# First pair's weight sums, one low part and four delays of side work re-ordered in a hybrid decoder kernel

## The chip, the cores and the metric

The kernel runs on one core of a Trainium2 chip. The metric is the device time of one execution in microseconds (us), as the median of several runs. The profile is one execution taken by the hardware profiler; its times count from the start of its span.

## What is computed

One layer of a decoder trunk on 520 tokens (512 new positions of one prompt and 8 single decode tokens) with a model width of 1024: a SwiGLU feed-forward of width 2816 (FFN1), a token mixer of retention and gated delta rule with four heads each, and a second feed-forward (FFN2).

```python
def layer(x, ...):
    x = x + 0.5 * rmsnorm(swiglu(rmsnorm(x, ffn1_pre_g), ...), ffn1_post_g)
    m, s_ret_new, s_gdn_new, s_conv_new = token_mixer(rmsnorm(x, mix_pre_g), ...)
    x = x + rmsnorm(m, mix_post_g)
    x = x + 0.5 * rmsnorm(swiglu(rmsnorm(x, ffn2_pre_g), ...), ffn2_post_g)
    return x, s_ret_new, s_gdn_new, s_conv_new

# token_mixer
proj = h @ w_in                       # q, k, v, gates of both branches
o_r, s_ret_new = retention_chunked(q, k, v, g_ret, s_ret)
cq, s_conv_new = short_conv(conv_in, s_conv, gdn_conv_w)
o_g, s_gdn_new = gated_delta_chunked(gq, gk, gv, g_gdn, beta, s_gdn)
y = sigmoid(gate_r) * (norm(o_r) @ w_ret_branch) + sigmoid(gate_g) * (norm(o_g) @ w_gdn_branch)
y = y @ w_out
```

## The kernel before

Activations lie with the model width on the partitions, as eight tiles of 128 x 520 (`x[k]`), and every product works on two halves of 260 tokens. Each product is made in three passes on TensorE from a high and a low part of both operands (`hi*hi`, `lo*hi`, `hi*lo`, lines 294, 295 and 296 of `passes`). The weights come from memory as fp32 into a pool of two raw buffers (`load_to`, line 188); ScalarE casts the high part (`whi`, line 254) and VectorE makes the low part (`wlo`, line 255), which frees the raw buffer. All weight loads are issued by SyncE (SP), in order, so a load that waits for a raw buffer holds up what is queued behind it.

Most of the gate and up products of the two FFNs are taken two row blocks at a time, as a pair, by a scheme of seven products in place of eight (`pair`, line 630, and `seven`). It needs sums of weight blocks. Of a pair, `load_to` loads `raw` (line 197), the left blocks of two sums, `s1` and `s3` (lines 198 and 199), and `a22` (line 200). GpSimd (POOL) then adds the right blocks with two accumulating DMAs (`add_sums`, line 215), `SUM_LAG` = 6 ticks later at the earliest. `split_seven` (line 257) turns each of the seven factors into a high part on ScalarE (line 272) and a low part on VectorE (line 273), both named `w`; one further sum, `s2` (line 268), is made on VectorE from `s1` and `raw`. The factors are used in the order raw, `s3`, `s2` (from `s1`), `a22` and so on. The banks of the products are emptied by ScalarE copies (`u` line 640, `q` line 643) and, for the plain products that precede the pairs, by VectorE (`t`, line 619).

The program is written in one order by a planner in the kernel: the main loop emits matmuls and calls `tick()` (line 148) about once every six matmuls. A tick issues due sums, prefetches weights, and resumes the generators of side work. `yield n` in a generator means "go on n ticks later". Each engine runs its own instructions in the order in which they were written and waits on semaphores where its inputs are not ready. The generators that matter here:

- `post` (line 442), for one half of the tokens at the end of FFN1 and of the mixer: per `k` a product `t` on VectorE (line 474), `x += t` on POOL (line 476), then the normalised input as a high part on ScalarE (line 383) and a low part on VectorE (`xhl`, line 384). In half 0 it also calls for one weight unit at `k` = 1 (`prefetch(True, 1)`), which puts a `wlo` into this chain. `acc` (line 395) and `y` (line 498) are the output sums and copies of the product that ends beside it.
- `pre_rms` (line 405): squares and their sum on VectorE (`sq`, line 415), then `inverse_rms`: column sums on TensorE (`ss`, line 356), a root on POOL (`rs`, line 351), and the row factor spread by TensorE (`rb`, line 362).
- `gates` (line 943): the decay and beta rows, with `gc` (line 988) on TensorE.
- `gdn_head` and `inverse` (line 1251): the inverse of a triangular 64 x 64 block per chunk, by a loop on `pack` (lines 1279 and 1280) and small products (`pV`, line 1303), and then a serial recurrence over chunks (`ks`, `pu`, `pS`, `go`).
- `ret_head` (line 1082): the retention recurrence; each step copies a state from PSUM (`st`, lines 1114 and 1118) that the next product `po` (line 1110) needs.
- `finish_head` (line 1335): transposes a head's result (`tr`, line 935), multiplies it by its gate (`sg`, line 1352) and splits it into `oh` (line 1353) and `ol` (line 1354).
- `decode_gdn` (line 1466): the decode tokens, with column sums `cs` (line 1371) of squares `gsq` (line 1483).
- `finish_decode` (line 1524), called by the main loop right before a branch product `br`: per head `df` (line 1530) on VectorE, the high part on ScalarE (`oh`, line 1531), the low part on VectorE (line 1532). The second half's `br` matmuls need them. The retention branch's first `br` is at 682.79 us in the trace, that of the delta branch at 763.38 us.

`token_factors` (line 551) makes the token-side sums of the seven products, once the next input is complete and its row factors are made (`rooted`).

## Time and profile before

| what | value |
|---|---|
| median of 3 runs (lowest, highest) | 1265.58 us (1261.89, 1268.35) |
| the profiled execution | 1265.27 us, of which the span of the trace is 1263.5 us |
| TensorE (PE) busy | 1214.7 us, 96% of the span |
| VectorE (DVE) busy | 864.6 us, 68% |
| ScalarE (ACT) busy | 538.5 us, 43% |
| GpSimd (POOL) busy | 255.9 us, 20% |
| mean granted clock of TensorE | 0.977 of 2.4 GHz |
| FFN1, mixer, FFN2 | to about 385 us, to about 880 us, to the end |

TensorE is busy nearly all the time, so a time can only fall where TensorE waits or where its clock is granted at the lower of its two levels. The waits of TensorE are the view to start from, and the timelines of the engines that it waits for tell why.

### The profile page before, as it was taken

What the parts mean: (1) busy time and instruction counts of PE and PEld (TensorE: products, weight loads), DVE (VectorE), ACT (ScalarE), POOL (GpSimd) and SP (SyncE); (2) the same over time, 40 slices, a digit from 0 to 9 for tenths busy, and PEclk for the clock granted to TensorE, in tenths of its full rate; (3) what the DMA queues carried; (4) which work ended last, traced back from release to release, by engine and by line L of the source; (5) the groups of instructions that cost most, each with busy time, mean ns of one, the idle gap of its engine ahead of it and who ended that gap; (6) DMA issues with size and microseconds to landing.
All of it is one profiled execution on the core that took longest, in us unless ns stands there. A gap on an engine that the chain in (4) does not pass through costs nothing.

```text
span 1263.5 us, 25461 instructions
## 1 busy us (share of the span) xinstructions
PE 1214.7 (96%) x10073; PEld 1203.5 (95%) x10073; DVE 864.6 (68%) x1911; ACT 538.5 (43%) x1117; POOL 255.9 (20%) x378
## 2 busy tenths in 40 slices
PE   8999999999999998899999999999989999999995
PEld 7999999999999998899999999999989999999995
DVE  8888888653347887878786766547878878852224
ACT  6566555432234654213334333334645655542210
POOL 4111112000023257136401112204211111100003
PEclk8999999999999899999999999999989999999997
DMA  5677777353332233232434554322377777524321
GB/s 176 178 185 193 184 180 176 94 157 92 91 94 68 87 101 112 77 95 85 129 123 123 197 179 151 118 84 84 122 201 180 178 178 184 144 78 160 92 76 68
DMA packets 76552, 166.60 MB, mean 132 GB/s; under 512 B 14481, under 2 KB 19953, under 8 KB 76433
## 3 DMA queue, kind: packets, MB, share of 16 engines
q1 hardware_dynamic: 64144, 140.69, 34.9%
q0 software_dynamic: 12288, 24.29, 11.3%
q8 instruction: 79, 1.29, 0.4%
q14 instruction: 41, 0.33, 0.1%
HBM read 155.24 MB, written 9.70 MB: 131 GB/s over the span
## 4 chain that ended last, share of the span: by engine, by line
PE 72%; DVE 13%; DMA 4%; issue 3%; ACT 3%; POOL 3%; SPq 0%; DVEq 0%; ACTq 0%; POOLq 0%
PE sv L294 9%; PE sv L295 9%; PE sv L296 9%; PE dn L295 7%; PE dn L294 7%; PE dn L296 7%; PE p L294 5%; PE p L295 5%; PE p L296 5%; DMA s<-gu_in 3%; DVE wlo L255 2%; PE br L294 1%; PE br L295 1%; PE br L296 1%; DVE cv L1049 1%
## 5 line engine op out<-in xcount | busy, mean ns | idle before, releaser
L294 PE MATMUL p<-xhl,whi 128*128 128x260 f32 x784 | 234.5, 299 | 0.0
L295 PE MATMUL p<-xhl,whi 128*128 128x260 f32 x784 | 224.8, 287 | 0.0
L296 PE MATMUL p<-xhl,wlo 128*128 128x260 f32 x784 | 224.4, 286 | 0.0
L295 PE MATMUL dn<-hl,whi 128*128 128x260 f32 x704 | 200.1, 284 | 2.7 <-DVE hl L608 2.7
L294 PE MATMUL dn<-hh,whi 128*128 128x260 f32 x704 | 200.1, 284 | 0.4 <-ACT hh L606 0.4
L296 PE MATMUL dn<-hh,wlo 128*128 128x260 f32 x704 | 199.5, 283 | 0.0
L255 DVE TENSOR_TENSOR wlo<-raw,whi 128x1024 fp32r<-128x1024 f32 (+2 forms) x133 | 156.8, 1192 | 56.9 <-ACT whi L254 56.7
L294 PE MATMUL sv<-th,w 128*128 128x260 f32 x592 | 169.0, 285 | 3.4 <-ACT u L640 3.2
L296 PE MATMUL sv<-th,w 128*128 128x260 f32 x592 | 168.3, 284 | 0.0
L295 PE MATMUL sv<-tl,w 128*128 128x260 f32 x592 | 168.1, 284 | 0.0
L254 ACT CAST whi<-raw 128x1024 fp32r<-128x1024 f32 (+2 forms) x133 | 128.1, 979 | 59.3 <-DMA raw<-dn_in 52.0
L294 PEld LDWEIGHTS p<-xhl,whi 128*128 128x128 f32 x784 | 151.4, 193 | 0.7
L295 PEld LDWEIGHTS p<-xhl,whi 128*128 128x128 f32 x784 | 151.6, 193 | 0.1
L296 PEld LDWEIGHTS p<-xhl,wlo 128*128 128x128 f32 x784 | 151.1, 193 | 0.0
L273 DVE TENSOR_TENSOR w<-s,w 128x512 fp32r<-128x512 f32 x148 | 101.4, 689 | 52.7 <-ACT w L272 51.0
L295 PEld LDWEIGHTS dn<-hl,whi 128*128 128x128 f32 x704 | 133.3, 189 | 3.3 <-DVE hl L608 3.3
L294 PEld LDWEIGHTS dn<-hh,whi 128*128 128x128 f32 x704 | 133.2, 189 | 0.6 <-ACT hh L606 0.6
L296 PEld LDWEIGHTS dn<-hh,wlo 128*128 128x128 f32 x704 | 133.5, 190 | 0.0
L294 PE MATMUL sv<-xhl,w 128*128 128x260 f32 x444 | 126.2, 284 | 5.2 <-DVE t L619 4.6
L215 POOL DMA_DIRECT2D s<-gu_in x74 | 65.0, 977 | 320.1 <-DMA s<-gu_in 152.0
L295 PE MATMUL sv<-xhl,w 128*128 128x260 f32 x444 | 125.7, 283 | 0.0
L296 PE MATMUL sv<-xhl,w 128*128 128x260 f32 x444 | 125.4, 282 | 0.0
(364 smaller groups left out, 2891.6 us busy)
## 6 DMA issues: line engine op xcount, KB each, us to landing
raw<-gu_in SPq DMA_DIRECT2D x50, 512.0 KB, 4.6
raw<-win_in SPq DMA_DIRECT2D x49, 512.0 KB, 3.6
s<-gu_in SPq DMA_DIRECT2D x74, 256.0 KB, 5.3
s<-gu_in POOLq DMA_DIRECT2D x74, 256.0 KB, 4.9
raw<-dn_in SPq DMA_DIRECT2D x32, 448.0 KB, 3.4
a<-gu_in SPq DMA_DIRECT2D x37, 256.0 KB, 5.5
raw<-dn_in SPq DMA_DIRECT2D x16, 512.0 KB, 3.5
x<-x SPq DMA_DIRECT2D x16, 260.0 KB, 5.4
```

What stands on the lines that cost most here:

```text
L215: self.nc.gpsimd.dma_start(out=out, in_=term, accum_op=ALU.add)
L254: self.nc.scalar.copy(hi[:, ks], t[:, ks])
L255: self.nc.vector.tensor_tensor(lo[:, ks], t[:, ks], hi[:, ks].bitcast(F32), ALU.subtract)
L273: nc.vector.tensor_tensor(w[:, 1], t[i], w[:, 0].bitcast(F32), ALU.subtract)
L294: mm(ps, hi[:, k, :], xh, start=first, stop=False, skip_group_check=more)
L295: mm(ps, hi[:, k, :], xl, start=False, stop=False, skip_group_check=more)
L296: mm(ps, lo[:, k, :], xh, start=False, stop=last, skip_group_check=more)
L1049: nc.vector.scalar_tensor_tensor(out=acc, in0=cin[:, j : j + SEQ], scalar=w[:, j : j + 1], in1=acc, op0=ALU.mult, op1=ALU.add)
```

## The change

The diff has three parts; the number of instructions on each engine is the same before and after.

1. A new `begin_pair` issues `s3`, `s1` and `a22` of a pair and enters its two sums, `s3` first. `token_factors` calls it for the first pair of each FFN as soon as the row factors are rooted, so before the raw loads that are still to come; for all other pairs `load_to` calls it behind the pair's raw load.
2. In `post` of half 0 the one forced prefetch moves ahead of the loop over `k`, and two ticks are let pass behind it.
3. Four delays of side work grow: `pre_rms` 1 to 3 ticks, `gates` 13 to 15, `inverse` 3 to 5, `decode_gdn` 6 to 11.

```diff
             if u[0] == "seven":
                 w, m = a[f"gu{u[1]}"], u[2]
                 t = self.raw.tile([P, KD, P], F32, tag="raw", name=self.name("raw"))
-                s1, s3, a22 = (self.slot(x, (P, KH, P)) for x in ("s1", "s3", "a22"))
                 nc.sync.dma_start(out=t, in_=w[2 * m])
-                nc.sync.dma_start(out=s1, in_=w[2 * m + 1, :, 0:KH])
-                nc.sync.dma_start(out=s3, in_=w[2 * m, :, 0:KH])
-                nc.sync.dma_start(out=a22, in_=w[2 * m + 1, :, KH:KD])
-
-                self.sums_due.append((self.now + SUM_LAG, self.raw_next, s1, w[2 * m + 1, :, KH:KD]))
-                self.sums_due.append((self.now + SUM_LAG, self.raw_next, s3, w[2 * m + 1, :, 0:KH]))
+                s1, s3, a22 = self.begun.pop((u[1], m), None) or self.begin_pair(u[1], m)
...
+    def begin_pair(self, f, m):
+
+        dma, w = self.nc.sync.dma_start, self.a[f"gu{f}"]
+        s1, s3, a22 = (self.slot(x, (P, KH, P)) for x in ("s1", "s3", "a22"))
+        dma(out=s3, in_=w[2 * m, :, 0:KH])
+        dma(out=s1, in_=w[2 * m + 1, :, 0:KH])
+        dma(out=a22, in_=w[2 * m + 1, :, KH:KD])
+
+        g = self.group[self.unit_list.index(("seven", f, m, 0))]
+        self.sums_due.append((self.now + SUM_LAG, g, s3, w[2 * m + 1, :, 0:KH]))
+        self.sums_due.append((self.now + SUM_LAG, g, s1, w[2 * m + 1, :, KH:KD]))
+        return s1, s3, a22
...
         while not self.leads:
             yield 1
-        yield 1
+        yield 3
         yield from self.inverse_rms(sq[0], r, plus)
...
             self.spawn(self.pre_rms(xs, r, plus_next))
+            self.prefetch(True, 1)
+            yield 2
         lag = 2
...
-            if not hf and k == 1:
-                self.prefetch(True, 1)
             yield 1
...
         while len(xs[1]) < KD or not self.rooted:
             yield 1
+
+        self.begun[f, plain] = self.begin_pair(f, plain)
...
-        yield 13
+        yield 15
...
         nc.vector.transpose(Tc, TTc)
-        yield 3
+        yield 5
...
-        yield 6
+        yield 11
         rs = self.const("gdr", [P, 64])
```

How the order changes, in three places. The changed kernel's line numbers are 5 to 10 higher, and buffer numbers differ.

SyncE at the start of FFN2, before: the raw loads, the first copies of `x` to memory, then the first pair's raw load with its `s1`, `s3` and `a22`.

```order
L208 DMA raw_11386<-gu_in 128x1024
L208 DMA raw_11392<-gu_in 128x1024
L208 DMA raw_11637<-gu_in 128x1024
L208 DMA raw_11643<-gu_in 128x1024
L778 DMA x_11329<-x_3858 128x520
L778 DMA x_11329<-x_3859 128x520
L778 DMA x_11329<-x_3860 128x520
L778 DMA x_11329<-x_3861 128x520
L197 DMA raw_11757<-gu_in 128x1024
L198 DMA s_1900_11758<-gu_in 128x512
L199 DMA s_1901_11759<-gu_in 128x512
L200 DMA a_1902_11760<-gu_in 128x512
```

The same place in the changed kernel, where lines 211, 212 and 213 are `s3`, `s1` and `a22`:

```order
L203 DMA raw_11398<-gu_in 128x1024
L203 DMA raw_11404<-gu_in 128x1024
L211 DMA s_1863_11631<-gu_in 128x512
L212 DMA s_1862_11630<-gu_in 128x512
L213 DMA a_1864_11632<-gu_in 128x512
L203 DMA raw_11655<-gu_in 128x1024
L203 DMA raw_11661<-gu_in 128x1024
L788 DMA x_11315<-x_3858 128x520
L788 DMA x_11315<-x_3859 128x520
L197 DMA raw_11746<-gu_in 128x1024
```

The three loads have moved ahead of two plain raw loads and of the pair's own raw load, and the copies of `x` are split otherwise around that.

VectorE at the start of half 0's chain between FFN1 and the mixer (`ms` is the mean square of the rows, line 349), before:

```order
L349 SCALAR_TENSOR_TENSOR ms_4787<-ss_4782,plus_12_135 65x4
L474 TENSOR_TENSOR t_4814<-y_3692,rb_4809 128x260
L474 TENSOR_TENSOR t_4823<-y_3849,rb_4809 128x260
L255 TENSOR_TENSOR wlo_4827<-raw_4683,whi_4826 128x1024
L474 TENSOR_TENSOR t_4846<-y_4026,rb_4809 128x260
L384 SCALAR_TENSOR_TENSOR xhl_4849<-x_3858,vec,xhl_4849 128x260
```

and in the changed kernel:

```order
L357 SCALAR_TENSOR_TENSOR ms_4787<-ss_4782,plus_12_135 65x4
L263 TENSOR_TENSOR wlo_4815<-raw_4683,whi_4814 128x1024
L484 TENSOR_TENSOR t_4840<-y_3692,rb_4809 128x260
L484 TENSOR_TENSOR t_4849<-y_3849,rb_4809 128x260
L484 TENSOR_TENSOR t_4858<-y_4026,rb_4809 128x260
L392 SCALAR_TENSOR_TENSOR xhl_4861<-x_3858,vec,xhl_4861 128x260
```

The low part has left the chain and stands ahead of its first `t`.

VectorE ahead of the retention branch's decode columns, before (`tr` is the transposed result of a delta head, `rdr` and `on_dec_r` belong to the decode tokens):

```order
L1235 COPY go_8644<-go_8903 128x128
L1352 SCALAR_TENSOR_TENSOR sg_8518<-tr_8909,vec,sg_8518 128x512
L1354 TENSOR_TENSOR ol_8915<-sg_8518,oh_8914 128x512
L1379 COPY rdr_8849<-cb_8926 128x32
L1456 TENSOR_TENSOR on_dec_r<-rdo,rdr_8849 128x32
L1388 COPY vrow_8938<-tr_1463_8936 32x128
L1215 SCALAR_TENSOR_TENSOR cv_5894<-ks_8954,neg_eg,cv_5894 128x128
L802 TENSOR_TENSOR gate_8963<-p_8871,rb_5236 128x260
L802 TENSOR_TENSOR gate_8963<-p_8872,rb_5236 128x260
L1530 SCALAR_TENSOR_TENSOR df_8966<-on_dec_r,vec,sgd_7894 128x8
```

and in the changed kernel:

```order
L1245 COPY go_8676<-go_8938 128x128
L1362 SCALAR_TENSOR_TENSOR sg_8505<-tr_8944,vec,sg_8505 128x512
L1364 TENSOR_TENSOR ol_8950<-sg_8505,oh_8949 128x512
L812 TENSOR_TENSOR gate_8960<-p_8862,rb_5248 128x260
L812 TENSOR_TENSOR gate_8960<-p_8863,rb_5248 128x260
L1540 SCALAR_TENSOR_TENSOR df_8963<-on_dec_r,vec,sgd_7859 128x8
```

Four small rows that stood between `ol` and the gates now stand earlier, so the head's `sg` and `ol` come right before `df`.

TensorE at the same place, before; the head's four transposes `tr` stand above these rows, with 26 rows between:

```order
L1214 MATMUL ks_8954<-S_8643,cv_5698 128x128
L294 MATMUL p_8871<-xhl_4961,whi_8654 128x260
L295 MATMUL p_8871<-xhl_4961,whi_8654 128x260
L296 MATMUL p_8871<-xhl_4961,wlo_8655 128x260
L294 MATMUL p_8872<-xhl_5104,whi_8654 128x260
L295 MATMUL p_8872<-xhl_5104,whi_8654 128x260
L296 MATMUL p_8872<-xhl_5104,wlo_8655 128x260
L294 MATMUL br_8988<-oh_8054,whi_8760 128x260
L295 MATMUL br_8988<-ol_8055,whi_8760 128x260
L296 MATMUL br_8988<-oh_8054,wlo_8761 128x260
L294 MATMUL br_8989<-oh_8054,whi_8760 128x260
```

and in the changed kernel:

```order
L945 MATMUL tr_8944<-cst,go_7899 128x128 x4
L302 MATMUL p_8862<-xhl_4973,whi_8632 128x260
L303 MATMUL p_8862<-xhl_4973,whi_8632 128x260
L304 MATMUL p_8862<-xhl_4973,wlo_8633 128x260
L302 MATMUL p_8863<-xhl_5104,whi_8632 128x260
L303 MATMUL p_8863<-xhl_5104,whi_8632 128x260
L304 MATMUL p_8863<-xhl_5104,wlo_8633 128x260
L302 MATMUL br_8985<-oh_8047,whi_8749 128x260
L303 MATMUL br_8985<-ol_8048,whi_8749 128x260
L304 MATMUL br_8985<-oh_8047,wlo_8750 128x260
L302 MATMUL br_8986<-oh_8047,whi_8749 128x260
```

The transposes have moved to nine matmuls before the second half's `br`, the first that reads the decode columns. At the delta branch's `br` they move likewise, from 33 matmuls before it to nine.

## Rows read from the trace of the kernel before

**Rows 1.** Waits of TensorE: engine, line, releaser, us in total, times, longest.

```profile
PE sv L294 <- DVE t L619: 4.6, 1, 4.6
PE ss L356 <- DVE acc L395: 3.6, 3, 1.8
...
PE cs L1371 <- DVE gsq L1483: 3.2, 1, 3.2
...
PE pV L1303 <- DVE pack L1279: 1.5, 1, 1.5
PE ss L356 <- DVE sq L415: 1.4, 2, 1.2
```

**Rows 2.** Windows: stretch, length, busy of PE, PEld, DVE, ACT, POOL, clock, DMA.

```profile
480.00:520.00 40.00, 35.14 (x299) 34.11 (x297) 33.75 (x98) 13.05 (x35) 21.35 (x49) 0.96 0.32 96
520.00:560.00 40.00, 35.67 (x290) 34.70 (x290) 34.45 (x121) 8.65 (x18) 9.48 (x11) 0.96 0.31 98
...
929.20:933.00 3.80, 3.80 (x19) 3.80 (x19) 3.06 (x6) 3.31 (x8) 0.00 (x0) 0.50 0.93 287
```

**Rows 3.** Chain of work that ended last: start, us, what.

```profile
47.40 0.66 POOL s L215
48.06 6.73 DMA s<-gu_in
...
909.67 4.23 DMA s<-gu_in
...
915.73 6.77 DMA s<-gu_in
```

**Rows 4.** Timeline of TensorE at three waits: start, us, work, idle before, releaser.

```profile
56.35 0.58 PE L294 MATMUL sv<-th,w 128*128 128x260 f32 x1 [2.50 <-ACT u L640]
...
637.25 0.59 PE L1303 MATMUL pV<-pack,AT 32*32 32x32 f32 x16 [0.81 <-DVE pack L1293]
...
928.85 0.56 PE L294 MATMUL sv<-xhl,w 128*128 128x260 f32 x1 [4.61 <-DVE t L619]
```

**Rows 5.** Timeline of VectorE around that pair.

```profile
923.23 0.69 DVE L273 TENSOR_TENSOR w<-s,w 128x512 fp32r<-128x512 f32 x1 [5.73 <-ACT w L272]
...
928.28 0.76 DVE L619 TENSOR_TENSOR t<-g,rb 128x260 f32<-128x260 f32 x2
```

**Rows 6.** Timeline of SyncE there: two plain raw loads, the first pair's raw load.

```profile
878.79 1.53 SPq L208 DMA_DIRECT2D raw<-gu_in  x2
...
909.29 0.33 SPq L197 DMA_DIRECT2D raw<-gu_in  x1
```

**Rows 7.** Timeline of ScalarE at FFN1's second pair.

```profile
54.89 1.14 ACT L272 CAST w<-s 128x512 fp32r<-128x512 f32 x2 [2.51 <-DMA s<-gu_in]
```

**Rows 8.** Timeline of VectorE in half 0's chain after FFN1.

```profile
372.58 1.66 DVE L255 TENSOR_TENSOR wlo<-raw,whi 128x1024 fp32r<-128x1024 f32 x1
```

**Rows 9.** Timeline of GpSimd in the same chain.

```profile
372.40 6.02 POOL L476 TENSOR_TENSOR x<-x,t 128x260 f32<-128x260 f32 x6 [2.33 <-DVE t L474]
```

**Rows 10.** Timeline of VectorE before the retention branch's product.

```profile
678.53 0.75 DVE L1352 SCALAR_TENSOR_TENSOR sg<-tr,vec,sg 128x512 f32<-128x512 f32 x1
...
680.58 0.18 DVE L1379 COPY rdr<-cb 128x32 f32<-128x32 f32 x1
...
682.63 0.79 DVE L802 TENSOR_TENSOR gate<-p,rb 128x260 f32<-128x260 f32 x2
683.34 0.22 DVE L1530 SCALAR_TENSOR_TENSOR df<-on_dec_r,vec,sgd 128x8 f32<-128x8 f32 x1
```

**Rows 11.** Timeline of TensorE there.

```profile
677.89 0.60 PE L935 MATMUL tr<-cst,go 128*128 128x128 f32 x4
...
682.79 0.28 PE L294 MATMUL br<-oh,whi 128*128 128x260 f32 x1
682.91 0.28 PE L295 MATMUL br<-ol,whi 128*128 128x260 f32 x1
...
683.84 0.38 PE L294 MATMUL br<-oh,whi 128*128 128x260 f32 x1 [0.53 <-ACT oh L1531]
```

More of the change, by code (lines that the diff above doesn't have):

```diff
@@ L135, in __init__ @@
         self.sums_due = []
+        self.begun = {}
         self.hold_sums = True
@@ L549, in first_units, with token_factors @@
         return banks
-    def token_factors(self, xs, gcol, F):
+    def token_factors(self, xs, gcol, F, f, plain):
         nc = self.nc
@@ L682, in pair @@
             return banks, at
-        self.spawn(self.token_factors(xs, gpre, F))
+        self.spawn(self.token_factors(xs, gpre, F, 1 if x_from is self.a["xT"] else 2, plain))
         lead = self.first_units(xs, "g", ((0,), (1,)) if x_from is self.a["xT"] else ((0, 1), (2, 3)))
```

## Prediction

> **What bounds the kernel now.** TensorE is busy 96% of the span, so the change can win only where it waits or runs at the lower of its two clock levels. I first read the list of what TensorE waited for [rows 1]: in single places of a few us at most. The largest is one wait of 4.6 us at the first pair of FFN2; then come single waits at FFN1's second pair [rows 4], at the decode sums `cs`, at `pV` of the inverses, and at the column sums `ss`. Second, the windows of the middle [rows 2]: from 480 to 560 us TensorE is busy 35.1 and 35.7 of 40 us, VectorE 33.8 and 34.5. So there VectorE is nearly as full as TensorE, and a wait that is taken away may come back at the next value that VectorE's queue delivers. Third, the granted clock: from 929.2 to 933.0 us, right behind the 4.6 us wait, it is 0.50, which is the level of 1.2 GHz [rows 2, 4]. There 19 matmuls took 3.80 us, 0.20 each; at the level of 2.4 GHz two of the same size stand 0.12 apart [rows 11]. Such a stretch costs 19 x 0.08 = 1.5 us beside the wait itself. I use this price for all such stretches.
>
> Last I read the timelines around each wait. At FFN2's first pair VectorE's `t`, which empties a bank that TensorE needs, stands at 928.28, behind a low part `w` at 923.23 that had waited 5.73 us [rows 5]. That goes back to a sum: the load went out at 909.67 and took 4.23 us, the second accumulating DMA started at 915.73 and took 6.77 [rows 3]. The loads stand in SyncE's queue behind the raw load at 909.29 [rows 6], which has to wait for a raw buffer to come free.
>
> **The change part by part.** The sum is made against the profiled execution, 1265.3 us, of which the span is 1263.5; it is 0.3 us below the median of the runs. A positive term is a gain.
>
> *First pair of FFN2.* The three loads now come right behind two plain raw loads that were issued from 878.79 on [rows 6], nearly 30 us earlier, and the two sums follow on POOL's queue right behind the row factors, some 15 us before the 915.73 of the trace. With 4.23 us for a load and 6.77 for a sum they are in place more than 5 us before the low part of 923.23 wants them. VectorE's 5.73 us of idling goes; its rows from 923.23 to 928.28 (5.05 us) then start at about 917.5, and `t` ends at about 923.3, with its second half. TensorE came there at 928.85 - 4.61 = 924.24 [rows 4], so the whole wait goes, and with it the slow stretch: 4.6 + 1.5 = 6.1. What is late next is the second pair: its raw load still hangs on a raw buffer, and TensorE will want its `s3` sum 6 us sooner. I expect it to arrive about in time. I take 6.0, with bounds 4.0 and 7.0. On POOL nothing but later sums stands behind these two, so the 0.66 us that it spends on each [rows 3] costs nothing.
>
> On the transfers themselves no row shows the pair's loads in the earlier place. The Trainium skill (DMA: Bandwidth & Descriptors, "Issuing engines are not separate DMA queues") says that transfers started by different engines end up on the same 16 DMA engines and interleave. By that rule the early loads would lengthen the plain raw loads beside them, and lighten the crowd at 909 to 918 us; the sum stays the same as long as each is hidden.
>
> *Second pair of FFN1.* `s3` is now summed before `s1`. TensorE waited 2.5 us for `u` until 56.35 [rows 4], and `u` stood on ScalarE behind two casts at 54.89, which waited for the `s3` sum, 48.06 + 6.73 = 54.79 [rows 3, 7]. As the first of the two, it is issued at 47.40 and lands after 4.23 to 6.73 us, at 51.6 to 54.1. I take the early end, since the long ones in the rows are always the second of two. But now `s1` lands at 54.8; `s2`, its cast and the copy `q` behind it need some 1.7 us (about 0.7, 0.6 and 0.4), to 56.5 (the cast by the two of rows 7, the others are estimates from it). TensorE, not stopped at 56.35 - 2.50 = 53.85, needs `q` twelve matmuls later, 53.85 + 12 x 0.12 = 55.3: a new wait of up to 1.2. So 2.5 - 1.2, and half of a slow stretch: 2.0, bounds 0.5 and 4.0. The other pairs have the same new order, with more lead.
>
> *FFN1 to mixer.* The low part of 1.66 us at 372.58 [rows 8] leaves half 0's chain for a place where VectorE was idle, waiting for `rb`. POOL then limits: six `x += t` took 6.02 us, 1.0 each, with hardly a break [rows 9]. So not the 1.66 comes back but about 1.1. `ss` for the next row factors comes two ticks later, 12 matmuls or 1.4 us, which covers its wait of 1.2 [rows 1]. With a third of a slow stretch, 1.1 + 1.2 + 0.5 = 2.8, bounds 1.0 and 4.9. The `gates` delay of two more ticks and that of `pre_rms` cancel: the gate sums stand as far behind their rows as before, so that wait stays.
>
> *The mixer's middle.* `decode_gdn` later by five ticks (30 matmuls, 3.6 us) covers the 3.2 us wait of `cs`, and `inverse` later by two (1.4 us) just covers the 1.5 us of `pV` [rows 1]. But the next waits in this stretch, on retention's `st` and the recurrence, end with VectorE's queue, which has hardly less to do before them. VectorE idles 6.2 and 5.6 us in the two windows [rows 2], and a gain can only come out of that. Bounds are 0 and 4.7 + 1.5 = 6.2. I take 2.8, a little under the middle.
>
> *A later inverse.* The same two ticks cover the 0.8 us wait of `pV` for `pack` at 637.25 [rows 4], and most of a slow stretch behind it: 2.0, bounds 0 and 2.3.
>
> *The cost: the heads end later.* The longer inverses push the last transposes `tr` of a delta head to nine matmuls before the `br` that needs the decode columns, in both branches. In the trace `tr` starts at 677.89, `sg` 0.64 later, and VectorE is through with `ol` at 680.58, 2.69 after `tr` [rows 10, 11]. Two gates and `df` follow: 0.71 from gate to `df`, 0.50 from `df` to `br` [rows 10, 11]. That makes 2.69 + 0.71 + 0.50 = 3.90 from `tr` to `br`. TensorE has work for 0.36 (the transposes) and nine matmuls, with the change of shape some 1.5 us in all. The wait is 2.4 us where it was 0.53 [rows 11]. Twice (3.9 - 1.5 - 0.5) = 3.8, and one slow stretch for the two: -5.3. The bounds are -1.0 (other work turns out to be between) and -9.8 (1.0 more at each place for rows in VectorE's queue ahead of `sg`, and a slow stretch and a half at each).
>
> The clock level behind a wait: the 4.6 us wait has a slow stretch behind it, the 0.53 us one has not [rows 4, 2, 11]. The Trainium skill (TensorE: Matmul & The Clock Gate, "Part 1: The HAM clock gate") states that the throttled level is the default and that activity releases it. By that rule each of the two new waits could bring its own slow stretch, 1.5 more than I count; no row here shows a wait at this place long enough to tell.
>
> *Mixer to FFN2.* As at FFN1, the low part leaves the chain. The wait on `acc` there is the longest of its kind, 1.8 [rows 1], but `acc` now comes in earlier among the `t`. I take 1.2, bounds 0 and 3.3.
>
> **The sum.** 6.0 + 2.0 + 2.8 + 2.8 + 2.0 - 5.3 + 1.2 = 11.5, so 1265.3 - 11.5 = 1253.8 us.
>
> **The rivals.**
>
> A. The middle of the mixer is VectorE's: the waits at `cs` and `pV` go, and come back at `st` and the recurrence in full, and the inverse at 637 us gains nothing either. For it speaks how full VectorE is [rows 2]; against it, that it idles 12 us there. Without 2.8 + 2.0: 1258.6.
>
> B. The sums of the second pairs take over. In FFN2 the second pair's `s3` sum, like the second of the rows (6.77), arrives some 2 us late, and in FFN1 the `q` wait brings a slow stretch: 3.5 less, 1257.3.
>
> C. The two `br` waits don't come, since some product stands between. Against it speaks the order. 1253.8 - 5.3 = 1248.5.
>
> D. The change doesn't do what it says at FFN2: the early sums don't help, because the pair's own raw load, still at 909.29 [rows 6], is what is waited for. Against it, the low part of the raw block was made before VectorE fell idle. Without 6.0: 1259.8.
>
> E. Slower than before: the late heads cost more than all else gains. The place is the two `br`. If VectorE is behind with its queue when `tr` is done, each wait grows by 1.5 to 3.9, and two slow stretches follow each (3.0): 2 x (3.9 - 0.5 + 3.0) = 12.8. The same lateness would take the mixer's gains. It decides from the point where the rest brings less than 12.8; with the low ends of the FFN terms, 4.0 + 0.5, it gives 1265.3 - 4.5 + 12.8 = 1273.6.
>
> **How the numbers follow.** I give the forecast 0.47, A 0.15, B 0.10, C 0.13, D 0.09, E 0.06. The most likely time is 1253.8. A measurement of this kernel can tell about 0.5%, 6.3 us, from no change, so "faster" means below 1259.3. Forecast, C, most of B and half of A lie below: 0.47 + 0.13 + 0.08 + 0.07 = 0.75. "Slower", above 1271.9, is most of E, 0.04; the rest, 0.21, is no change. The range reaches from 1245, a few us under C since several terms have more room above than below, to 1261, just over D.
>
> **What would show it.** Right: no wait of TensorE on `t` of line 619 at the start of FFN2, and the pair's sums landed before 910 us; the casts at FFN1's second pair some 3 us earlier, with a wait of about 1 us on `q` behind them; no wait on `cs`; waits of about 2.4 us at both `br`, on the `oh` of `finish_decode`. Wrong: waits on `st` or `ks` that together are longer than before by as much as `cs` and `pV` lost (A), a wait of the FFN products on `u` or `t` one pair later (B), `br` waits near 0.5 (C), the old 5.7 us idling of VectorE at FFN2's first pair (D).

## The result, and the profile after

The changed kernel is a little slower: 1268.67 us in the median of 22 runs (1261.72 to 1274.31), beside 1265.36 us for 22 runs of the kernel before on the same chip. The ratio is 1.0029, with an interval of 1.0015 to 1.0042, so 1.9 to 5.3 us were lost where 11.5 were forecast as gained. The profiled execution of the changed kernel took 1265.6 us (span 1263.8), 3 us below its own median, so its trace shows that much less of the loss. Two executions of this study, one of the kernel before (1611 us) and one of f3_dec (2364 us), lie far above all others and are left out of every median and ratio.

First the waits of TensorE in the changed kernel; the columns are those of [rows 1]:

```profile
PE sv L302 <- ACT q L653: 5.3, 2, 3.5
PE br L302 <- ACT oh L1541: 4.3, 2, 2.2
...
PE po L1120 <- DVE st L1128: 3.0, 1, 3.0
PE po L1120 <- POOL TT L1298: 2.7, 1, 2.7
...
PE po L1121 <- DVE sT L1104: 2.0, 1, 2.0
PE sv L302 <- ACT u L650: 1.8, 1, 1.8
PE sp L1438 <- DMA sd<-sret_in: 1.7, 1, 1.7
...
PE cs L1374 <- DVE rdo L1455: 1.2, 1, 1.2
```

The rows that the change aimed at are gone: `sv` on `t` (4.6), `cs` on `gsq` (3.2) and `pV` on `pack` (1.5) of [rows 1] have no successor of more than 0.3 us. But the list is not shorter. FFN products now wait 5.3 us for `q` and 1.8 for `u` (0.2 and 3.2 before). `po` of the retention waits 7.7 us in three rows (3.2 before), `br` waits 4.3 us where it waited 1.1, and a wait on the transfer of `sd` is new.

To see in which stage this counts, the trace is cut at four groups of row factors `rb`, which TensorE spreads: those of half 0 and of half 1 behind FFN1, those ahead of FFN2, and those of half 0 behind FFN2. Before, then after, their rows (count, shortest/median/longest in ns, first to last start in us; the last row holds half 1's group too):

```profile
L362 PE MATMUL rb<-cst,rs x8: 220/275/276, 370.9 to 371.6; 65*128 65x65 f32 x8
...
L362 PE MATMUL rb<-cst,rs x8: 275/275/323, 382.8 to 383.7; 65*128 65x65 f32 x8
...
L362 PE MATMUL rb<-cst,rs x16: 221/275/276, 897.9 to 899.5; 65*128 65x65 f32 x16
...
L362 PE MATMUL rb<-cst,rs x16: 275/275/422, 1240.8 to 1250.9; 65*128 65x65 f32 x16
```

```profile
L370 PE MATMUL rb<-cst,rs x8: 221/275/275, 371.0 to 371.7; 65*128 65x65 f32 x8
...
L370 PE MATMUL rb<-cst,rs x8: 275/275/324, 381.3 to 382.1; 65*128 65x65 f32 x8
...
L370 PE MATMUL rb<-cst,rs x16: 221/275/275, 899.7 to 901.4; 65*128 65x65 f32 x16
...
L370 PE MATMUL rb<-cst,rs x16: 275/370/430, 1240.7 to 1251.3; 65*128 65x65 f32 x16
```

The stages are the differences of these starts, in us (the experiments are told below). The mixer's column holds the way into the mixer and out of it too:

| kernel | FFN1, to half 0's rb | from there to half 1's | mixer, to the rb ahead of FFN2 | FFN2, to half 0's rb | span |
|---|---|---|---|---|---|
| before | 370.9 | 11.9 | 515.1 | 342.9 | 1263.5 |
| after | 371.0 | 10.3 | 518.4 | 341.0 | 1263.8 |
| after, profiled again (e4_after) | 371.6 | 10.3 | 524.0 | 340.8 | 1269.1 |
| pairs alone (e1_pairs) | 370.5 | 12.0 | 513.9 | 340.7 | 1259.4 |
| delays alone (e3_delays) | 372.4 | 11.9 | 522.8 | 341.2 | 1271.5 |
| inverse alone (e9_inv) | 372.0 | 12.0 | 515.8 | 342.0 | 1264.2 |
| gates alone (f1_gates) | 373.8 | 12.0 | 517.9 | 342.1 | 1268.5 |
| gates and inverse (f2_gatesinv) | 372.0 | 11.9 | 524.9 | 339.4 | 1270.5 |
| decode alone (f3_dec) | 370.5 | 12.0 | 516.9 | 341.7 | 1263.5 |
| after without inverse (e6_noinv) | 371.4 | 10.2 | 515.8 | 341.6 | 1261.4 |
| two early in FFN2 (e8_twoearly) | 371.9 | 12.0 | 514.1 | 332.7 | 1253.9 |
| two early in both, low part (e12_bothtwo) | 369.8 | 10.3 | 513.4 | 333.5 | 1249.3 |

Each row is one profile, and the scatter is large: the same changed kernel has 518.4 and 524.0 us in the mixer, the profile of f1_gates lies 5 us above that kernel's median, and the kernels whose FFN2 is that of before (before, e3, e9, f1, f2, f3) have 339.4 to 342.9 there. So the 1.9 us that FFN2 gained here are within the scatter. FFN1 itself gained nothing, and the 1.6 us behind it come from the low part's move: the second column falls from 11.9 or 12.0 to 10.2 or 10.3 in every kernel that has it, and in no other. The mixer lost 3.3, in the second profile of the same kernel 8.9. So there are two questions: why FFN2 gave at most 1.9 and not 6, and what the mixer lost.

**FFN2.** The rows of the changed kernel there, engine by engine, with the idle time before an instruction and its releaser in brackets: SyncE (raw loads of the second and of the third pair), GpSimd's sums of the first and of the second pair, VectorE, ScalarE and TensorE.

```profile
920.21 0.33 SPq L197 DMA_DIRECT2D raw<-gu_in  x1
...
925.90 0.33 SPq L197 DMA_DIRECT2D raw<-gu_in  x1
...
899.11 1.86 POOL L223 DMA_DIRECT2D s<-gu_in  x2
925.16 0.86 POOL L223 DMA_DIRECT2D s<-gu_in  x1 [24.19 <-DMA s<-gu_in]
926.62 0.89 POOL L223 DMA_DIRECT2D s<-gu_in  x1 [0.60 <-issue]
...
935.12 0.69 DVE L276 SCALAR_TENSOR_TENSOR s<-s,raw 128x512 f32<-128x512 f32 x1 [3.38 <-DMA s<-gu_in]
...
935.90 0.62 ACT L280 CAST w<-s 128x512 fp32r<-128x512 f32 x1 [4.69 <-DVE s L276]
...
931.26 0.39 PE L302 MATMUL sv<-th,w 128*128 128x260 f32 x1 [1.82 <-ACT u L650]
...
936.85 0.59 PE L302 MATMUL sv<-th,w 128*128 128x260 f32 x1 [3.52 <-ACT q L653]
```

The first pair's sums go out at 899.11, long before they are wanted, and nothing waits for them. The second pair's raw load goes out at 920.21, and its two sums at 925.16 and 926.62. Beside them the third pair's raw load and three more loads run from 925.90 on. The chain of work that ended last shows what the raw load waited for, and the second sum:

```profile
918.96 1.24 DVE wlo L263
...
920.63 3.97 DMA s<-gu_in
...
926.62 8.48 DMA s<-gu_in
```

The raw load goes out as soon as the `wlo` of a plain block is made, which frees its raw buffer; the change moves nothing there. The second sum took 8.48 us, so it lands at 935.10, and VectorE's `s`, ScalarE's cast, its `q` and TensorE follow, with a wait of 3.52 us. The wait of 1.82 us before it, on `u`, comes from the first sum in the same way (4.5 us to landing). Both stand one pair later than the 4.61 us of [rows 4]. TensorE's clock fell behind the first of them and stayed low through the second. The window (columns as in [rows 2]) shows 0.50, 1.2 GHz, with 31 matmuls in it, where [rows 2] had 19:

```profile
932.40:942.60 10.20, 6.68 (x31) 6.38 (x31) 5.74 (x12) 4.36 (x10) 1.74 (x2) 0.50 0.65 138
```

In before, the second pair's raw load stood at 916.92 and the third's at 928.43, 11.5 us apart, and the second pair's second sum went out at 925.41. Their rows, and the time of that sum from issue to landing:

```profile
916.92 0.33 SPq L197 DMA_DIRECT2D raw<-gu_in  x1
...
928.43 0.33 SPq L197 DMA_DIRECT2D raw<-gu_in  x1
...
925.41 0.89 POOL L215 DMA_DIRECT2D s<-gu_in  x1 [0.49 <-ACT w L272]
...
DMA to landing us min/median/max: 4.6/4.6/4.6
```

There the third pair's loads followed 3.0 us behind the sum, which took 4.6 us. Now the raw loads are 5.7 us apart, since the first pair's raw buffer comes free earlier when that pair no longer waits, and the same sum takes 8.48. So the wait of [rows 4] had also hidden the next pair's late sums, and kept the third pair's loads off them.

**The mixer.** From 600 to 800 us, before and then after:

```profile
600.00:800.00 200.00, 198.13 (x1698) 195.56 (x1697) 141.28 (x412) 73.31 (x160) 36.77 (x63) 0.99 0.46 149
```

```profile
600.00:800.00 200.00, 192.08 (x1651) 188.87 (x1650) 137.31 (x403) 70.73 (x155) 32.40 (x57) 1.00 0.46 149
```

TensorE idled 7.9 us there instead of 1.9, at a granted clock of 1.00. Four waits make up 7.3 of it: `sp` on `sd` 1.7, `cs` on `rdo` 1.2, and the two at `br`, whose rows answer to [rows 11] and [rows 10]:

```profile
679.98 0.60 PE L945 MATMUL tr<-cst,go 128*128 128x128 f32 x4
...
683.84 0.38 PE L302 MATMUL br<-oh,whi 128*128 128x260 f32 x1 [2.17 <-ACT oh L1541]
...
680.62 0.75 DVE L1362 SCALAR_TENSOR_TENSOR sg<-tr,vec,sg 128x512 f32<-128x512 f32 x1
...
683.34 0.22 DVE L1540 SCALAR_TENSOR_TENSOR df<-on_dec_r,vec,sgd 128x8 f32<-128x8 f32 x1
```

From `tr` to `br` it is 683.84 - 679.98 = 3.86 us (3.90 forecast), and the wait is 2.17 us (2.4 forecast).

The two windows of [rows 2] in the changed kernel:

```profile
480.00:520.00 40.00, 34.98 (x283) 33.73 (x282) 36.83 (x106) 12.89 (x37) 20.14 (x48) 0.87 0.39 112
520.00:560.00 40.00, 36.20 (x311) 35.42 (x311) 31.81 (x113) 9.54 (x18) 8.46 (x11) 1.00 0.27 80
```

TensorE is busy 71.2 of 80 us, as before (70.8), though the waits on `cs` and `pV` are gone.

### The profile page after: what moved, and what is told of

Its sections match the earlier page's. It is cut to its first block, busy times and chain, and to the rows that moved or that the text cites. A ratio compares the mean times of both kernels' runs of the same rounds, so it can differ in the third digit from the quotient of the medians.

```text
span 1263.8 us, 25476 instructions
## 1 busy us (share of the span) xinstructions
PE 1210.4 (96%) x10073; PEld 1196.3 (95%) x10073; DVE 862.6 (68%) x1911; ACT 544.7 (43%) x1117; POOL 249.6 (20%) x378
## 4 chain that ended last, share of the span: by engine, by line
PE 71%; DVE 15%; DMA 4%; ACT 4%; issue 3%; POOL 1%; SPq 1%; DVEq 0%; ACTq 0%; POOLq 0%
PE sv L302 10%; PE sv L303 10%; PE sv L304 10%; PE dn L303 7%; PE dn L302 7%; PE dn L304 7%; PE p L302 4%; PE p L304 4%; PE p L303 4%; DVE wlo L263 3%; DMA s<-gu_in 2%; DVE cv L1059 1%; PE br L302 1%; PE br L303 1%; PE br L304 1%
## 5 line engine op out<-in xcount | busy, mean ns | idle before, releaser
L302 PE MATMUL p<-xhl,whi 128*128 128x260 f32 x784 | 232.3, 296 | 0.7 <-DVE S L1236 0.7
L303 PE MATMUL p<-xhl,whi 128*128 128x260 f32 x784 | 222.4, 284 | 0.5 <-DVE xhl L392 0.5
L302 PEld LDWEIGHTS p<-xhl,whi 128*128 128x128 f32 x784 | 148.7, 190 | 1.3 <-DVE S L1236 0.9
L303 PEld LDWEIGHTS p<-xhl,whi 128*128 128x128 f32 x784 | 148.9, 190 | 0.7 <-DVE xhl L392 0.7
```

The source lines that it names most:

```text
L302: mm(ps, hi[:, k, :], xh, start=first, stop=False, skip_group_check=more)
L303: mm(ps, hi[:, k, :], xl, start=False, stop=False, skip_group_check=more)
```

## The experiments

All changes are against the kernel named; ratios are against the kernel before, run on the same chip, with their 95% interval.

### Which part does what: e1, e2, e3, e4

**e1_pairs**, the kernel before with the first part alone (begin_pair, `s3` first, first pair of each FFN early):

```diff
+    def begin_pair(self, f, m):
...
+        self.begun[f, plain] = self.begin_pair(f, plain)
```

> The kernel before with part 1 alone (early first pair, s3 ahead of s1 in every pair). Theory 1, the wait moves from the first pair's t to the second pair's second sum, now s1, on which s2 and the copy q hang: no gain, 1264 to 1268 us; at FFN2's start no wait on t, but a wait on q or u of 2 to 5 us one pair later, and at FFN1's second pair a wait on q in place of u. Rival, the pairs do gain what was forecast (8 us) and the delays alone eat it: 1257 to 1259 us and no wait over 1.5 us at the second pair of FFN2.

Measured: 1260.02 us, ratio 0.9963 (0.9949 to 0.9978).

**e2_lowpart**, the kernel before with the low part's move alone:

```diff
+            self.prefetch(True, 1)
+            yield 2
...
-            if not hf and k == 1:
-                self.prefetch(True, 1)
```

> The kernel before with part 2 alone (the one low part ahead of half 0's chain, two ticks behind it). Theory 1: about 1 us gain at each of the two transitions, 1262 to 1264 us, the rest of the program as before. Rival: the two ticks and the earlier acc give it back, 1265 to 1267 us.

Measured: 1263.05 us, 0.9983 (0.9963 to 1.0002), the range of theory 1.

**e3_delays**, the kernel before with the four delays alone:

```diff
-        yield 1
+        yield 3
         yield from self.inverse_rms(sq[0], r, plus)
...
-        yield 13
+        yield 15
...
         nc.vector.transpose(Tc, TTc)
-        yield 3
+        yield 5
...
-        yield 6
+        yield 11
         rs = self.const("gdr", [P, 64])
```

> The kernel before with part 3 alone (the four longer delays). Theory 1: the middle of the mixer gains 3 to 6 us by 600 us and the late heads lose 7 us or more between 608 and 775 us, so 1266 to 1270 us, with waits of about 2.2 us at both br. Rival, the delays gain as forecast (2 to 3 us in sum): 1262 to 1263 us.

Measured: 1273.14 us, 1.0065 (1.0039 to 1.0092).

**e4_after**, the changed kernel once more beside these three:

> The changed kernel as it is, a second time, for a second profile beside the three parts. Theory 1: 1266 to 1270 us, with the waits at the second pair of FFN2 and at br again; what differs between the two profiles of one kernel tells which waits vary from run to run. Rival: other places than these carry the loss, then they are seen here.

Measured: 1268.11 us, 1.0025 (1.0009 to 1.0042).

So the first part gains 0.37%, 4.7 us, the second perhaps 2, and the delays alone lose 0.65%, 8.2 us. All the loss is theirs. The prediction had them at about +0.7 us: 2.8 and 2.0, less 5.3, with 1.2 for `ss`. Two expectations missed: the time of e1_pairs lies between its two ranges, with the waits of theory 1, and e3_delays lost more than theory 1 gave it.

The trace of e1_pairs, without any delay, has FFN2's waits too. SyncE's raw loads of the second and third pair, the second sum in the chain of work, and TensorE:

```profile
915.37 0.33 SPq L197 DMA_DIRECT2D raw<-gu_in  x1
...
921.06 0.33 SPq L197 DMA_DIRECT2D raw<-gu_in  x1
...
922.12 8.53 DMA s<-gu_in
...
929.22 0.39 PE L302 MATMUL sv<-th,w 128*128 128x260 f32 x1 [3.58 <-ACT u L650]
...
932.40 0.58 PE L302 MATMUL sv<-th,w 128*128 128x260 f32 x1 [1.44 <-ACT q L653]
```

Again the raw loads are 5.7 us apart, the sum takes 8.53 us, and 5.0 us of waits follow, though the mixer ran as before (513.9 us). The sum started 3.3 us earlier than before (922.12 for 925.41) and still landed 0.7 us later.

### FFN2's second pair: e5, e8, e10, e12, f4

**e5_s1first**, the changed kernel with `s1` loaded and summed before `s3`:

```diff
-        dma(out=s3, in_=w[2 * m, :, 0:KH])
         dma(out=s1, in_=w[2 * m + 1, :, 0:KH])
+        dma(out=s3, in_=w[2 * m, :, 0:KH])
...
-        self.sums_due.append((self.now + SUM_LAG, g, s3, w[2 * m + 1, :, 0:KH]))
         self.sums_due.append((self.now + SUM_LAG, g, s1, w[2 * m + 1, :, KH:KD]))
+        self.sums_due.append((self.now + SUM_LAG, g, s3, w[2 * m + 1, :, 0:KH]))
```

> The changed kernel with the sums and loads in the old order, s1 ahead of s3. Theory 1, whichever sum comes second runs under the next pair's loads and is the slow one: the wait of TensorE at the second pairs is on u for s3 again (2 to 4 us at FFN1 and at FFN2), and none on q. Rival, the slow one is s1 in either order: waits on q as in the changed kernel.

Measured: 1275.34 us, one run, with waits as theory 1 had them, the second one longer. TensorE's waits in FFN1 and FFN2 are both on `u` now, which is made from `s3`:

```profile
57.61 0.39 PE L302 MATMUL sv<-th,w 128*128 128x260 f32 x1 [3.49 <-ACT u L650]
...
945.41 0.58 PE L302 MATMUL sv<-th,w 128*128 128x260 f32 x1 [6.71 <-ACT u L650]
```

Whichever sum is the second is the late one, and TensorE needs `s3` first. That speaks for the new order, by one run: the wait at 57 us is 3.49 here, and 1.74 and 2.25 in the two profiles of the changed kernel.

**e8_twoearly**, the first part alone, with FFN2's second pair begun early as well:

```diff
         self.begun[f, plain] = self.begin_pair(f, plain)
+        if f == 2:
+            self.begun[f, plain + 1] = self.begin_pair(f, plain + 1)
```

> Part 1 alone, and in FFN2 the second pair is begun early as well, right behind the first. Theory 1, the first pair's gain is lost since the second pair's sums run under the third pair's loads: with them out of the way the waits of 3.6 and 1.4 us at 929 and 932 us go, 3 to 6 us faster than part 1 alone, 1254 to 1257 us. Rival, VectorE's or ScalarE's queue limits the start of FFN2: waits of the same size on other releasers, 1259 to 1261 us.

Measured: 1255.22 us, 0.9907 (0.9886 to 0.9928), as theory 1 had it. GpSimd issues four sums in a row at the start of FFN2, and TensorE's waits of 3.58 and 1.44 us shrink to one of 0.66:

```profile
897.42 3.66 POOL L223 DMA_DIRECT2D s<-gu_in  x4
...
929.79 0.38 PE L302 MATMUL sv<-th,w 128*128 128x260 f32 x1 [0.66 <-ACT q L655]
```

FFN2 takes 332.7 us, 8 us less than in e1_pairs and 10.2 less than before. This shows what the first part lacked: not the early first pair, which works, but the second.

**e10_twolow**, e8_twoearly with the low part's move of e2_lowpart:

> Part 1 with FFN2's second pair begun early too, and part 2; no delay changed. If the parts add: 1265 x 0.9907 x 0.9983, so 1251 to 1254 us. Rival, part 2's earlier acc and the early sums meet and give 2 us back: 1255 to 1257 us.

Measured: 1256.06 us, 0.9934 (0.9908 to 0.9961): the rival's range, and no gain by the low part's move that can be told.

**e12_bothtwo**, as e10_twolow, with two pairs early in FFN1 too:

```diff
         self.begun[f, plain] = self.begin_pair(f, plain)
-        if f == 2:
-            self.begun[f, plain + 1] = self.begin_pair(f, plain + 1)
+        self.begun[f, plain + 1] = self.begin_pair(f, plain + 1)
```

> As the fourth part of the study with two early pairs and part 2, but in FFN1 as well the second pair is begun early. If the sums of the second pair are what TensorE waits for at 56 us, that wait of 2 to 2.5 us goes: 1 to 4 us faster than with FFN2's second pair alone, 1248 to 1252 us. Rival, at the start of FFN1 the loads meet the first loads of all and come no earlier: no difference, 1252 to 1254 us.

Measured: 1251.68 us (1251.08 to 1252.10), 0.9901 (0.9870 to 0.9932), in the first range. It beats both kernels. The longest single wait left in TensorE's list is the old one of the mixer on `cs`; at the pairs 0.7 us is left:

```profile
PE cs L1382 <- DVE gsq L1494: 3.2, 1, 3.2
```

**f4_bothonly**, the same without the low part's move:

> The kernel before with the new order of a pair's loads and with both pairs of FFN1 and of FFN2 begun early, without the low part's move. Against the run of the same with the low part's move (1251.68 us): if that move is worth the 1 to 2 us that its run alone had suggested, 1253 to 1255 us; if it brings nothing once the sums come in time, 1251 to 1252.5 us. In both cases at least 0.7% faster than before.

Measured: 1254.31 us, 0.9903 (0.9871 to 0.9935). The medians lie as the first theory had it, but they are of two chips, and the ratios are the same. What the low part's move brings to the whole stays open: by e2_lowpart it is between nothing and 0.4%.

### Which delays lose, and why: e6, e7, e9, e11, f1, f2, f3

**e6_noinv**, the changed kernel with the inverse's delay taken back (`yield 5` to `yield 3`):

> The changed kernel with inverse's delay back at 3 ticks; all else as changed. Theory 1, the longer inverses push the heads' ends against the branch products and cost most of what is lost from 608 to 775 us: waits at br near 0.5, 1260 to 1263 us. Rival, decode_gdn's delay costs it: the loss there stays, 1266 to 1269 us.

Measured: 1263.80 us, 0.9969 (0.9956 to 0.9981), between the two ranges. The waits at `br` are 1.79 and 0.75 us, not both near 0.5.

**e7_nodec**, the changed kernel with the decode's delay taken back (`yield 11` to `yield 6`):

> The changed kernel with decode_gdn's delay back at 6 ticks; all else as changed. Theory 1 (inverse costs the time): the 2 to 3 us wait at cs comes back and the br waits of 2.2 us stay, 1268 to 1271 us. Rival (decode_gdn costs it): 1261 to 1264 us, br waits smaller.

Measured: 1268.32 us, 1.0025 (1.0008 to 1.0043), as the changed kernel and as theory 1 had it; the waits at `br` stay at 2.18 and 2.19 us.

**e9_inv**, the kernel before with the inverse's delay alone (`yield 3` to `yield 5`):

> The kernel before with inverse's delay alone at 5 ticks. Theory 1 (the heads' lateness costs): slower than before by 2 to 6 us, 1267 to 1271 us, with waits over 1 us at the first br; the 0.8 us wait of pV at 637 us gone. Rival, inverse's delay costs only together with the other delays: 1263 to 1266 us.

Measured: 1265.93 us, 1.0007 (0.9990 to 1.0024), the rival's range.

So the same two ticks cost 7.6 us in the changed kernel (1.0029 against 0.9969) and nothing alone. Another of the delays must take part, and e7_nodec says that it isn't the decode's. The last runs decide that.

**f1_gates**, the kernel before with `pre_rms` (1 to 3) and `gates` (13 to 15):

> The kernel before with two of the four delays alone: the row factors' pre_rms two ticks later and the gates two ticks later; inverse and decode_gdn as before. In the order of TensorE the last transposes of a delta head stand 21 rows ahead of br's second half, as with the inverse's delay alone. Theory (the delays draw on one slack of about 33 rows at br, and only their sum overdraws it): waits at both br under 1 us, time within 0.3% of before, 1262 to 1269 us. Rival (these two are bad by themselves, and the inverse's only added to it): br waits of 1.5 us or more and at least 0.4% slower, 1270 us or more.

Measured: 1265.20 us, 0.9999 (0.9976 to 1.0022), as the theory had it.

**f2_gatesinv**, f1_gates with the inverse's delay:

> The kernel before with three of the four delays: pre_rms, gates and inverse, decode_gdn as before. The last transposes stand nine rows ahead of br's second half, as in the changed kernel. Theory (one slack, overdrawn by the sum of these two groups): br waits of about 2.2 us twice, which were 0.53 before; with what follows them the time is 0.4 to 0.8% longer, 1270 to 1276 us, as with all four delays. Rival (the decode's delay is a needed part of the loss): within 0.3% of before, 1262 to 1269 us, whatever the br waits are.

Measured: 1273.92 us, 1.0067 (1.0045 to 1.0089), as the theory had it.

**f3_dec**, the kernel before with the decode's delay alone:

> The kernel before with decode_gdn five ticks later alone. If the cover of the cs wait of 3.2 us is worth its time, 1262 us or less (0.25% faster or better); if it comes back at the next waits on VectorE's queue in the mixer's middle, or if the decode's later end takes it back at br, within 0.2% of before, 1263 to 1268 us. No wait of over 1 us at br by either, since the heads' transposes stand where they did.

Measured: 1264.92 us, 0.9994 (0.9975 to 1.0013), the second range.

Two groups of delays that cost nothing each (the interval of f1_gates reaches 0.2% to either side) lose 8.5 us together. The waits at `br` say how, first those of f1_gates, then of f2_gatesinv:

```profile
PE br L294 <- ACT oh L1531: 1.5, 2, 0.7
```

```profile
PE br L294 <- ACT oh L1531: 4.4, 2, 2.2
```

Beside it, how many rows stand in TensorE's order between the last `tr` of a delta head and the second half of `br`, which wants the decode columns, at the retention branch's and at the delta branch's `br`:

| kernel | delays in it | rows between tr and br | waits at br, us | ratio |
|---|---|---|---|---|
| before | none | 36, 33 | 0.53, 0.53 | 1 |
| f3_dec | decode | 36, 33 | 0.52, 0.53 | 0.9994 |
| e9_inv | inverse | 21, 21 | 0.75, 0.74 | 1.0007 |
| f1_gates | pre_rms and gates | 21, 21 | 0.73, 0.74 | 0.9999 |
| f2_gatesinv | pre_rms, gates, inverse | 9, 9 | 2.18, 2.18 | 1.0067 |
| e3_delays | all four | 9, 9 | 2.18, 2.19 | 1.0065 |
| e6_noinv, with parts 1 and 2 | pre_rms, gates, decode | 21, 21 | 1.79, 0.75 | 0.9969 |

Both groups draw on one stock of some 35 rows. The first 12 to 15 cost 0.2 us a place, the next 12 cost 1.4 us. The last line shows that rows of TensorE are not the whole stock: with 21 of them the first wait is 1.79 us and not 0.75. There the later decode has put its state rows `sd` on VectorE between the head's `ol` and the gates; e11_finish4, told below, has them at the same place:

```profile
683.74 1.13 DVE L1417 SCALAR_TENSOR_TENSOR sd<-rb,gkn,sd 128x128 f32<-128x128 f32 x4
```

In f2_gatesinv, the same product of the main loop starts 0.2 us later than before at 660 us, 3.9 later at 685, 3.8 at 760 and 7.3 at 785, and the spans of the two profiles differ by 7.0: so 7.2 us are lost at the two places. The waits themselves are 1.65 us more each. Behind the second, the clock was at 0.50 for 3.4 us, which the same length behind the first was not:

```profile
771.40:774.80 3.40, 3.40 (x18) 3.40 (x17) 2.33 (x6) 2.62 (x4) 0.25 (x1) 0.50 0.03 7
688.00:691.40 3.40, 3.40 (x30) 3.40 (x30) 1.83 (x6) 2.63 (x8) 0.00 (x0) 1.00 0.00 0
```

There 18 matmuls took the time of 30, 1.4 us. Behind the first wait the clock stayed at 1.00, but a wait of 0.9 us on `AT` stands ahead of it. That makes 5.6 of the 7.2 us; the rest was not traced further.

f3_dec shows the other half of the matter. The `cs` wait of [rows 1] fell from 3.2 to 0.4 us, and these rows of TensorE's waits grew:

```profile
PE pV L1303 <- DVE pack L1293: 4.6, 2, 3.8
...
PE po L1110 <- POOL TT L1288: 3.1, 1, 3.1
```

Before, `pV` had 1.5 and 0.8, and `po` on `TT` 0.9; `po` on `st` stayed (2.0, now 2.1). The main products of f3_dec stood 4.0 us ahead of before's at 495 us, 8.9 at 509, and 1.0 behind at 584: what the later decode gave at `cs`, and more, was lost again within 75 us.

**e11_finish4**, the changed kernel with the head's end moved two ticks earlier, which takes `tr` further away from `br`:

```diff
-        yield 6
+        yield 4
         g = self.vec[:, V_RNORM
```

> The changed kernel with finish_head's delay at 4 ticks in place of 6, which puts the last transposes 24 and 21 matmuls ahead of the br that reads the decode columns, not 9. Theory 1, the 2.2 us waits at both br come from that distance: both fall below 1 us, 1264 to 1266 us. Rival, they come from the decode sums or from VectorE's queue as a whole: waits stay near 2 us, 1267 to 1270 us.

Measured: 1268.25 us, 1.0026 (1.0010 to 1.0042). The two `br` waits fell:

```profile
PE br L302 <- ACT oh L1541: 2.4, 2, 1.6
```

They lost 1.9 of 4.3 us, but the time did not follow; it is in the rival's range. The first is still 1.62 us with 24 rows between, as in e6_noinv with `sd` on VectorE ahead of it; the second is 0.74 with 21. The changed kernel and this one can be told apart by about 2.5 us, so this run doesn't confirm that `br` is the larger part of the loss, nor does it rule it out. That rests on f1_gates, e9_inv and f2_gatesinv.

## Why the prediction was wrong

Two steps failed. The larger is that the four delays were given gains of 2.8 and 2.0 us in the mixer beside their cost at the heads' end; alone they lose 8.2 us. The smaller is that FFN2's second pair was expected "about in time"; it came 5.3 us late.

**FFN2's first pair** (forecast 6.0 us, bounds 4 to 7). The mechanism held: the sums landed before 910 us (the second went out at 899.75 and took 8.3), and the wait on `t` fell from 4.6 to 0.3. The step that failed is "its raw load still hangs on a raw buffer ... I expect it to arrive about in time". It came 5.3 us late, in two waits, with a longer slow stretch behind. Rival B had this mechanism, with 2 us for it. The sizes were at hand: from raw load to second sum [rows 6, 3] it is 915.73 + 6.77 - 909.29 = 13.2 us, and that span goes with the buffer, not with the demand; in the changed kernel it was 935.10 - 920.21 = 14.9. TensorE wanted the second pair 6 us sooner, and its raw load was 1.6 us sooner in e1_pairs (915.37 for 916.92), in the changed kernel 3.3 later. FFN2 as a whole gained 1.9 us in these two profiles, which the scatter allows to be nothing.

That the second pair's second sum became longer (8.48 and 8.53 us for 4.6) was not foreseen either. What is new is that the third pair's four loads, on another engine's queue, start beside it and not 3.0 us behind. The Trainium skill (DMA: Bandwidth & Descriptors, "Issuing engines are not separate DMA queues") says that such transfers interleave on the same DMA engines; these traces agree. But the second sum of [rows 3], 6.77 us, also had the next pair's four loads from 1.2 us behind its start on, so the time is not set by their number alone, and no run changes the neighbours by themselves. The prediction used the rule for the first pair, where nothing hung on it, and not for the second.

**FFN1's second pair** (2.0). The wait moved from `u` to `q` as described: 1.74 us where up to 1.2 was forecast, since the second sum took 7.32 us and landed at 55.55, not 54.8. No gain is shown: up to half 0's `rb` FFN1 took 370.9 us before and 371.0 after, and the other kernels with the FFN1 of before scatter there from 370.5 to 373.8.

**FFN1 to mixer, and mixer to FFN2** (2.8 and 1.2). Of these 4.0 us, 1.2 were put down to the later `pre_rms` and 2.8 to the low part, which alone measured 2.2 us, with an interval from -0.3 to 4.7. That fits, and next to nothing does as well. At its first place the move works: from half 0's to half 1's `rb` 1.6 us are gained, where 1.1 was forecast for the chain. But the `rb` ahead of the mixer starts at 404.2 us for 405.1, so 0.9 is left there. The wait of `ss` on `sq` [rows 1] is gone in e1_pairs too, which has no later `pre_rms`, so its 1.2 us can't be put down to that delay.

**The mixer's middle** (2.8, bounds 0 and 6.2). Rival A was right in what it gave: the decode's delay alone brings nothing (0.9994), and its 2.8 us at `cs` stand at `pV` and at `po` on `TT` in f3_dec. It was not right in the place: `st` stayed at 2.1 us and `ks` fell, and `TT` is made by GpSimd, not by VectorE. The step that failed is "I take 2.8, a little under the middle"; it was the lower end. VectorE idles 12 us there [rows 2], but none of it was turned into time; why not was not traced.

**A later inverse** (2.0). Also rival A: alone 1.0007. In e9_inv the wait of 0.8 us on `pack` at 637 us is gone, and `po` waits 1.7 us on `TT` where it waited 0.9.

**The heads' end** (-5.3). The best of the terms: waits of 2.17 and 2.18 for 2.4, and 7.2 us in f2_gatesinv, within the bounds. (The far bound is added wrongly: 3.8 + 2.0 + 4.5 is 10.3, not 9.8.) But it was set off against gains of 4.8 from the same delays that don't exist. The prediction counted one slow stretch for the two waits. In the six profiles with waits of 2.16 to 2.19 us at both places (after, e3, e4, e5, e7, f2), seven of the twelve waits have a stretch at 0.50 right behind; in f2_gatesinv one of two has it, and in the first profile of the changed kernel none. The Trainium skill (TensorE: Matmul & The Clock Gate, "Part 1: The HAM clock gate") states that the throttled level is the default and that activity releases it. That each of the two waits could bring a slow stretch agrees with these traces; that each does, does not.

**What was missed.** The state load `sd` and the decode sums on `rdo` made TensorE wait 1.7 and 1.2 us in the changed kernel, on no step of the prediction. In the two kernels with the delays but without the early pairs these two are 0.2 and 1.2 (e3_delays), and none and 0.5 (f2_gatesinv). The wait on `sd` is absent from e6_noinv and from e7_nodec, the whole change without one of the delays. What makes `sd` late in the whole change was not tried.

**The rivals.** A and B both came true in the main; together they would have given 1258.6 + 3.5 = 1262.1, and B's 3.5 was too small. C and D were wrong: the waits came, and the early sums helped. E had the right sign and place, the two `br`, but 12.8 us for them where f2_gatesinv lost 8.5, and waits of 3.9 where 2.2 were measured; its sign came out all the same, since the rest of the delays brought nothing.

In sum, for the parts measured alone: forecast 8.0 for the pairs, 0.7 for the delays and 2.8 for the low part; measured 4.7, -8.2 and 2.2. They add up to -1.3, and the whole measured -3.7 (0.29%), which the intervals allow. The direction turned on the delays, the smallest sum of the three, made of terms of opposite sign.

## What to carry to other kernels

A wait that is removed at the first of a row of equal steps is worth only what the second step's inputs allow: work out when those inputs come by their own chain (buffer, load, sum), and move them early too; here that turned a gain of 4.7 us into one of 12.

Delays of side work that cost nothing each can share one stock of slack. Count, at the place where their results are needed, how many instructions of the waiting engine lie between, and add up all that draw on it before costing one. Look too at what else the delays put into the delivering engine's queue there: four rows `sd` made 0.75 us into 1.79.

Don't count a gain at one wait while the engines that serve it are nearly full, until you have seen what releases the next wait: here 2.8 us at `cs` came back at `pV` and `po`.

## What the hardware showed

A plain load of one `s` block took 3.97 and 4.23 us in the chains shown. The accumulating DMA into such a block took 4.6 us as the second pair's second sum of before, 6.77 as the first pair's, and 8.48 and 8.53 with the next pair's loads starting beside it. Of the four issued in a row in e8_twoearly the shortest took 4.0 us, the median was 9.1 and the longest 11.4. One size so has a range of nearly three to one, and it is longest behind others of its kind.

TensorE's clock did not fall behind every wait of the same length: at 688 us, behind 2.18 us, it stayed at 2.4 GHz, and at 771 us, behind 2.18 us again, it was at 1.2 GHz. Over six profiles it was at 1.2 GHz right behind seven of twelve such waits.
